# Norms over heads in float32r sums with a logarithm, in place of float32 column sums with Newton steps

## The chip, the cores and the metric

The kernel runs on one core of a Trainium2 chip. Its time is the device time of one execution in microseconds (us), taken as the median of the runs shown; lower is better. A core has five engines that matter here: TensorE (PE in the profile, with its weight loads as PEld), VectorE (DVE), ScalarE (ACT), GpSimd (POOL) and SyncE (SP, which issues most transfers). Each engine runs its own instructions strictly in order.

## The reference

Three layers act on 512 positions of 2048 features in float32. The change lies in the first one, which mixes three kinds of heads, all of 64 features. Cut to what the change touches:

```python
# rwkv: 12 heads, worked in six pairs of 128 features
kk = kk / jnp.maximum(jnp.sqrt(jnp.sum(jnp.square(kk), axis=-1, keepdims=True)), 1e-12)
...                                   # decay, rates a, a recurrence over positions gives y
mu = jnp.mean(y, axis=-1, keepdims=True)
var = jnp.mean(jnp.square(y - mu), axis=-1, keepdims=True)
y = ((y - mu) * lax.rsqrt(var + GN_EPS)) * gn_g + gn_b + bonus
# stick-breaking attention: 12 heads, six pairs
q = _rms(heads(q), qn_g) * (HEAD_DIM ** -0.5)      # x * rsqrt(mean(x*x) + 1e-6) * g
k = _rms(heads(k), kn_g)
# rates of rwkv
logw = -softplus(-(w0 + tanh(wd) @ w_up)) - 0.5;  a = sigmoid(a0 + ad @ a_up)
```

So four times per layer kind a tile of 128 features (two heads) by 512 positions needs one over the root of a sum of squares over 64 features: for the rwkv keys, for the rwkv output's norm, for q and for k of the stick-breaking heads. With six pairs each that is 24 tiles. The other two layers (an S5 layer with chunked attention, and a forgetting attention) are not touched.

## The kernel before

Activations lie with features on partitions and positions along the free axis, so a sum over a head goes across partitions and is done on PE. All large weights (the "dense" products into the tiles `big`) are split in a high and a low float32r part, and each slice of 128 features takes three products (L311, L312, L313) of 128x512. The high part `wh` is a copy on ACT (L181; in some stages on POOL, L280), the low part `wl` a subtraction on DVE (L163). Four slices share a buffer, there are four buffers, and the splitting runs about three buffers ahead of PE.

The order on every engine is the order in which the program emits instructions; no scheduler changes it. Work that isn't dense is written as generators. `pump(n)` takes n steps of the running streams, and one step of the main stream is the three dense products of one slice; `beside(main, side, wait)` lets a side generator do one piece after each step of the main one, from step `wait` on. So a bare `yield` in a side generator stands for "three dense products go in between". Whatever a piece emits for ACT and DVE lands in those engines' queues at that point, behind all that was emitted before.

`head_rs` (L374) is the norm: four float32 products per tile (L383) against the 128x2 matrix `heads` put the sums for 128 positions at a time on partitions; `ops` scales them, `newton` does the inverse root in 10 tiny DVE instructions (L411 to L416), L392 spreads it over 64 columns, and after `lag` steps four transposes (L406) bring it back to the layout of the data, in PSUM; `use` multiplies. It is called at three places:

- `decay` in the start of each rwkv pair (`front`): first the two rates (float32 products `wdad` by `up`, L1403, two Tanh, a scan L1407, two Exp), then the key's norm.
- `norm` of a pair's output, which runs beside the next pair's start; its last act is to add the bonus and write to `yd`.
- `stick_front`: while v is projected, q's and k's norms in one call; v then goes through transposes (L1767).

In an rwkv pair PE then needs, in this order, the products L1493 (keys by queries in chunks), L1525, a triangular inverse that begins at L1652 and goes on at L1662 to L1680, and L1539 and later lines for the state. The inverse's input `xb` comes from two DVE transposes L1641 and L1642 after four ACT copies `xa`. The input of L1539 (`GT`, `KM`, `UV`) comes from ACT copies behind L1493 of the next pair. The key `tm` of the next pair is projected, multiplied on DVE (`tm<-big,rs`), shifted (ACT `omu`, DVE L1355) and squared in between. In a stick-breaking step PE computes scores (L752), ACT and DVE build `sbl` and `sbe` (two Exp, one Ln, L1824 and L1825), PE sums them (L1846), and so on, with the next pair's `stick_front` and dense products pumped in between.

Of the kernel before, what the change touches and what calls it, by code (L numbers as in the profile page):

```python
# [9 lines left out]
F32 = mybir.dt.float32  # L10
F32R = mybir.dt.float32r
I32 = mybir.dt.int32
BF16 = mybir.dt.bfloat16
AF = mybir.ActivationFunctionType
OP = mybir.AluOpType
# [12 lines left out]
EXTRA_RATE = (.4,.5,.5,.5)  # L28
RWKV_WAIT = (5,(2,2,4))
STICK_WAIT = (8,6)  # L30
HEAD_LAG = (3,5,7)
RWKV_STEPS = (0,0,0,(13,6),4,4,3,3,3,1,1)
# [109 lines left out]
class Kern:  # L142
# [49 lines left out]
    def constants(self, tmp):  # L192
# [31 lines left out]
        V = nc.vector  # L224
        V.scalar_tensor_tensor(self.cen_r, blk, -1.0 / 64, self.ident, op0=OP.mult, op1=OP.add)
        self.heads = c.tile([128, 2], F32, name="heads")
        V.tensor_copy(self.heads, blk[:, 0:128:64])
        self.ident_r = mr("ident_r")
        self.copy(self.ident_r, self.ident)
        self.one = c.tile([128, 1], F32, name="one")  # L230
        nc.vector.memset(self.one, 1.0)
# [131 lines left out]
    def small(self):  # L363
        return self.ps.tile([128, 512], F32, name="sm", bufs=4)

    def ring(self, pool, name, bufs):
        return lambda dt=F32: pool.tile([128, T], dt, name=name, bufs=bufs)
# [5 lines left out]

    def head_rs(self, pool, ring, sqs, ops, use, lag=4):  # L374


        nc = self.nc
        V = nc.vector
        n = 8 * len(sqs)
        ps = self.early()  # L380
        for i, sq in enumerate(sqs):
            for b in range(4):
                nc.tensor.matmul(ps[:, 8 * i + 2 * b:8 * i + 2 * b + 2], sq[:, 128 * b:128 * b + 128], self.heads,  # L383
                                 start=True, stop=True)
        small = lambda name, dt=F32: pool.tile([128, n], dt, name=name, bufs=2)
        m = small("hm")
        ops(m, ps[:, 0:n])
        y = self.newton(m, small("hy", I32), small("ht"))
        wide = []
        for i in range(len(sqs)):  # L390
            wide.append(ring())
            V.tensor_copy(wide[i].rearrange("p (g c) -> p g c", c=64),  # L392
                          y[:, 8 * i:8 * i + 8, None].to_broadcast([128, 8, 64]))
        for _ in range(lag):
            yield
        for i, t in enumerate(wide):
            ps = self.early()
            for b in range(4):
                n = slice(128 * b, 128 * b + 128)
                self.spread(ps[:, n], t[:, n])  # L400
            use(i, ps)
            yield
# [971 lines left out]
    def rwkv(self, pool, tm, yd, acts, rs):  # L1374
# [9 lines left out]
        def front(j):  # L1384
# [5 lines left out]
            k = yield from self.shifted(tm, 6 + j, acts, rs)  # L1390
            kk, sq, Pi, P, b = (tm() for _ in range(5))
            self.copy(kk, k, scale=self.pv("k_k", j))
            self.act(sq, kk, AF.Square)
            PT = pool.tile([128, 8], F32, name="PT", bufs=2)

            ks = []

            def decay():

# [4 lines left out]
                for t, ps, bias in zip((Pi, b), both, ("w0", "a0")):  # L1404
                    self.act(t, ps, AF.Tanh, bias=self.half[bias][:, j:j + 1], scale=0.5)
                V.tensor_scalar(Pi, Pi, 0.5, 0.5, op0=OP.mult, op1=OP.add)
                V.tensor_tensor_scan(P, self.reset.rearrange("p c t -> p (c t)"), Pi, 0.0, OP.mult, OP.add)  # L1407
                self.act(Pi, P, AF.Exp, scale=C05)
                self.act(P, P, AF.Exp, scale=-C05)
                yield  # L1410

                def use(_, y):
                    self.mul(kk, kk, y)
                    self.mul(RKV[:, :, 1, 1:64], ch(kk)[:, :, 1:64], ch(P)[:, :, 0:63])
                    V.tensor_copy(RKV[:, :, 1, 0:1], ch(kk)[:, :, 0:1])
                yield from self.head_rs(pool, tm, [sq], lambda m, s: V.tensor_scalar(m, s, 1e-24, None, op0=OP.max), use, HEAD_LAG[0])

# [38 lines left out]
        def norm(j, g, bon, gate):  # L1456
# [5 lines left out]
            gc = self.sums(self.small(), hi, lo, self.cen_r)  # L1462
            yc, sq = tb(), tb()
            self.copy(yc, gc)
            self.act(sq, yc, AF.Square)

# [6 lines left out]
            for _ in range(3):  # L1473
                yield
            yield from self.head_rs(pool, tb, [sq], lambda m, s: V.tensor_scalar(m, s, 1.0 / 64, 64e-5, op0=OP.mult,
                                                                            op1=OP.add), use, HEAD_LAG[1])

# [261 lines left out]
    def stick_front(self, tm, j, acts, rs, pool=None):  # L1739
# [7 lines left out]
        for out, c, gain in ((q, 33 + j, self.qg8), (k, 39 + j, self.pv("kn_g"))):  # L1747
            t = yield from self.projected(tm, c, acts, rs)
            sq = tm()
            self.act(sq, t, AF.Square)  # L1750
            x.append((out, t, gain, sq))

        def use(i, y):
            out, t, gain, _ = x[i]
            V.scalar_tensor_tensor(out, t, gain, y, op0=OP.mult, op1=OP.mult)
            if pool:
# [3 lines left out]
            self.projected(tm, 45 + j, acts, rs),  # L1760
            self.head_rs(self.fr, tm, [y for _, _, _, y in x],
                         lambda m, s: V.tensor_scalar(m, s, 1.0 / 64, 1e-6, op0=OP.mult, op1=OP.add), use, HEAD_LAG[2]), STICK_WAIT[0])

# [171 lines left out]
```

## Time and profile before

| | |
|---|---|
| median of 3 runs | 3011.6 us (3009.29 to 3014.44) |
| the profiled execution | 3016.27 us, of which span 3014.0 us |
| PE busy | 2944.0 us, 98% |
| PEld busy | 2418.0 us, 80% |
| DVE busy | 1619.1 us, 54% |
| ACT busy | 1146.2 us, 38% |
| POOL busy | 373.5 us, 12% |
| mean granted TensorE clock | 0.98 |

The rwkv pairs take about 60 to 600 us of the span, the stick-breaking steps about 600 to 900 us; the norms that change lie there alone. PE is the engine that is hardly ever idle, so time is gained or lost by PE's own work, by what PE waits for, and by the clock that it is granted (1.00 in a row is 2.4 GHz, 0.50 is 1.2 GHz).

### The profile page before, as it was taken

Reading aid. Unit: us, or ns where it says so; the run is one execution under the profiler, and the core shown is the slowest. Engines: PE = TensorE matmul, PEld = TensorE weight load, DVE = VectorE, ACT = ScalarE, POOL = GpSimd, SP = SyncE. Lnnn points to the kernel's source line nnn. Section 1 sums busy time; section 2 is a strip of 40 time slices with the busy share of each in tenths; the row PEclk is TensorE's granted clock in tenths of the full one; section 3 lists DMA queues with packets and bytes.
Section 4 is the critical chain, followed back from the end, with each engine's and each line's share of the span. In section 5 each row is a group of like instructions: output and inputs, shape, how many; then the busy total and the mean of one; then the engine's idle time right before and its main releaser. Section 6 shows DMA issues by size and latency. Waiting matters only on the chain. (4 is left out here: it accounts for less than half of the span.)

```text
span 3014.0 us, 42793 instructions
## 1 busy us (share of the span) xinstructions
PE 2944.0 (98%) x16068; PEld 2418.0 (80%) x16068; DVE 1619.1 (54%) x3253; ACT 1146.2 (38%) x2062; POOL 373.5 (12%) x819
## 2 busy tenths in 40 slices
PE   8999999999999999999999999999999999999998
PEld 6777777778887887788888887888888888888887
DVE  6655555477767675555454455354444444444534
ACT  5443443354454223223344454233333232333432
POOL 0111111013764000211100000001101010100001
PEclk9998999999999999999999999999999999999999
DMA  4211111222234555454433325543332333223443
GB/s 156 67 56 59 57 57 59 78 81 85 94 96 158 158 182 180 135 159 157 138 105 104 102 85 177 146 130 109 101 105 96 98 96 96 95 91 95 148 121 119
DMA packets 195296, 334.01 MB, mean 111 GB/s; under 512 B 29696, under 2 KB 44672, under 8 KB 193936
## 3 DMA queue, kind: packets, MB, share of 16 engines
q1 hardware_dynamic: 193808, 327.08, 34.9%
q0 software_dynamic: 1280, 4.20, 0.4%
q8 instruction: 126, 2.06, 0.3%
q14 instruction: 82, 0.67, 0.1%
HBM read 289.55 MB, written 42.70 MB: 110 GB/s over the span
## 5 line engine op out<-in xcount | busy, mean ns | idle before, releaser
L311 PE MATMUL big<-hi,wh 128*128 128x512 f32 x3424 | 1375.5, 402 | 4.6 <-ACT hi L181 3.9
L312 PE MATMUL big<-lo,wh 128*128 128x512 f32 x3424 | 1347.5, 394 | 2.3 <-DVE lo L163 2.3
L313 PE MATMUL big<-hi,wl 128*128 128x512 f32 x3424 | 1347.0, 393 | 0.7 <-DVE wl L163 0.6
L163 DVE TENSOR_TENSOR wl<-wr,wh 128x512 fp32r<-128x512 f32 x884 | 621.9, 714 | 709.9 <-ACT wh L181 707.6
L311 PEld LDWEIGHTS big<-hi,wh 128*128 128x128 f32 x3424 | 650.1, 190 | 150.2 <-issue 11.1
L181 ACT ACTIVATE wh<-wr 128x512 fp32r<-128x512 f32 x835 | 515.6, 626 | 657.1 <-PE big L312 520.2
L313 PEld LDWEIGHTS big<-hi,wl 128*128 128x128 f32 x3424 | 649.6, 190 | 141.2 <-DVE wl L163 2.7
L312 PEld LDWEIGHTS big<-lo,wh 128*128 128x128 f32 x3424 | 650.8, 190 | 132.8 <-DVE lo L163 5.6
L683 ACT ACTIVATE pm<-pm,mx 128x128 f32<-128x128 f32 (+3 forms) x128 | 70.5, 551 | 178.6 <-DVE mx L679 178.6
L1235 POOL TENSOR_SCALAR dm<-cb,cq 128x128 f32<-128x128 f32 (+1 forms) x64 | 42.4, 663 | 598.4 <-DVE mx L677 580.1
L163 DVE TENSOR_TENSOR tm<-big,rs 128x512 f32<-128x512 f32 x85 | 58.5, 689 | 73.8 <-PE big L313 73.7
L176 ACT ACTIVATE sq<-xn 128x512 f32<-128x512 f32 (+1 forms) x47 | 28.8, 614 | 161.5 <-DVE xn L163 161.5
L181 ACT ACTIVATE pt<-sm 128x512 f32<-128x512 f32 (+3 forms) x96 | 43.4, 526 | 62.7 <-PE sm L711 62.7
L163 DVE TENSOR_TENSOR xn<-big,xr 128x512 f32<-128x512 f32 (+1 forms) x50 | 33.3, 667 | 53.2 <-PE big L313 46.3
L181 ACT ACTIVATE qk<-tm 128x512 fp32r<-128x512 f32 x32 | 20.2, 633 | 96.3 <-DVE tm L163 48.2
L1615 POOL MEMSET xi<- 64x16 f32 x6 | 0.7, 119 | 448.0 <-DVE xi L1614 448.0
L280 POOL CAST wh<-wr 128x512 fp32r<-128x512 f32 x49 | 34.2, 698 | 128.3 <-PE big L312 81.7
L163 DVE TENSOR_TENSOR pl<-sm,pt 128x512 fp32r<-128x512 f32 (+1 forms) x48 | 25.9, 596 | 44.3 <-ACT pt L181 44.3
L689 DVE TENSOR_SCALAR pm<-pm,sm 128x128 f32<-128x128 f32 (+3 forms) x128 | 43.3, 400 | 1.1
L163 POOL TENSOR_TENSOR xn<-xn,rs 128x256 f32<-128x256 f32 x12 | 8.6, 756 | 284.0 <-ACT rs L181 284.0
L1371 DVE SCALAR_TENSOR_TENSOR tm<-big,rs 128x512 f32<-128x512 f32 x33 | 22.7, 689 | 36.5 <-PE big L313 36.5
L311 PE MATMUL sm<-hi,wh 128*128 128x512 f32 x80 | 32.6, 408 | 8.7 <-ACT wh L181 8.7
(449 smaller groups left out, 3118.2 us busy)
## 6 DMA issues: line engine op xcount, KB each, us to landing
wr<-w_in_odd SPq DMA_DIRECT2D x256, 256.0 KB, 3.3
wr<-w_in SPq DMA_DIRECT2D x228, 256.0 KB, 3.1
wr<-w_in_even SPq DMA_DIRECT2D x192, 256.0 KB, 3.5
wr<-w_out SPq DMA_DIRECT2D x64, 256.0 KB, 3.8
wr<-w_out_even SPq DMA_DIRECT2D x64, 256.0 KB, 3.5
wr<-w_out_odd SPq DMA_DIRECT2D x64, 256.0 KB, 3.4
xr<-x SPq DMA_DIRECT2D x48, 256.0 KB, 3.0
yl<-y SPq DMA_DIRECT2D x45, 256.0 KB, 4.2
```

The costliest lines, as they stand in the source:

```text
L163: (eng or self.nc.vector).tensor_tensor(out, a, b, op=op)
L176: self.nc.scalar.activation(out, x, f, scale=scale)
L181: self.nc.scalar.activation(out, x, AF.Copy, scale=scale)
L280: self.nc.gpsimd.tensor_copy(wh, wr)
L311: nc.tensor.matmul(ps, wh[:, i], hi, start=(k == 0), stop=False)
L312: nc.tensor.matmul(ps, wh[:, i], lo, start=False, stop=False)
L313: nc.tensor.matmul(ps, wl[:, i], hi, start=False, stop=(k == n - 1))
L683: nc.scalar.activation(d, d, AF.Exp, bias=mx[:, b:b + 1], accum_out=sm[:, b:b + 1])
L689: V.tensor_scalar(d, d, sm[:, b:b + 1], None, op0=OP.mult)
L1235: nc.gpsimd.tensor_scalar(D[:, QOFF[b]:QOFF[b] + n], cb[:, 0:n], -1.0, cq[:, b, h:h + 1], op0=OP.mult, op1=OP.add)
L1371: self.nc.vector.scalar_tensor_tensor(t, ps, scale, rs, op0=OP.mult, op1=OP.mult)
L1615: G.memset(X.rearrange("p i c -> p (i c)")[:, 0:256:17], 1.0)
```

## The change

`squares` makes, beside the square, its float32r high part (a second ACT instruction). `head_rs` makes the low part on DVE, sums over heads with two float32r products of 128x512 (`sums`) against a 128x128 matrix of ones or of 1/64 per head, so that the sum lies at once on all partitions of its head. The inverse root is exp(-ln(s)/2): ACT Ln from PSUM with the floor as bias (for the keys first a DVE max), ACT Exp, and after the lag one Newton step of three DVE instructions of 128x512, the second of which reads the sums from PSUM. `use` then multiplies by a tile in SBUF. The transposes, the tiny Newton steps and the spread copy are gone. The rates' part of `decay` becomes a generator `rates` that runs between the low part and the sums, in pieces with bare yields. The constants of the layout change with it.

```diff
-RWKV_WAIT = (5,(2,2,4))
-STICK_WAIT = (8,6)
-HEAD_LAG = (3,5,7)
+RWKV_WAIT = (2,(2,2,4))
+STICK_WAIT = (2,6)
+HEAD_LAG = (2,5,8)
...
-        self.heads = c.tile([128, 2], F32, name="heads")
-        V.tensor_copy(self.heads, blk[:, 0:128:64])
+        self.mean_r = mr("mean_r")
+        self.copy(self.mean_r, blk, scale=1.0 / 64)
...
+    def squares(self, ring, x):
+
+        sq, hi = ring(), ring(F32R)
+        self.act(sq, x, AF.Square)
+        self.copy(hi, sq)
+        return sq, hi
+
+    def head_rs(self, ring, sqs, mat, op, floor, use, aside=()):
+
+
+        V = self.nc.vector
+        parts = []
+        for sq, hi in sqs:
+            lo = ring(F32R)
+            self.sub(lo, sq, hi.bitcast(F32))
+            parts.append((hi, lo))
+        yield from aside
+        for _ in range(HEAD_LAG[0]):
             yield
...
+        first = []
+        for (sq, _), (hi, lo) in zip(sqs, parts):
+            first.append((self.sums(self.early(), hi, lo, mat), sq, ring()))
+            yield
+        for ps, y, _ in first:
+            if op == OP.add:
+                self.act(y, ps, AF.Ln, bias=self.floors[floor])
+            else:
+                V.tensor_scalar(y, ps, floor, None, op0=op)
+                self.act(y, y, AF.Ln)
+        for _, y, _ in first:
+            self.act(y, y, AF.Exp, scale=-0.5)
+        for _ in range(HEAD_LAG[len(sqs)]):
+            yield
+        for i, (ps, y, t) in enumerate(first):
+            V.scalar_tensor_tensor(t, y, -0.5, y, op0=OP.mult, op1=OP.mult)
+            V.scalar_tensor_tensor(t, ps, floor, t, op0=op, op1=OP.mult)
+            V.scalar_tensor_tensor(y, t, 1.5, y, op0=OP.add, op1=OP.mult)
+            use(i, y)
             yield
...
-            def decay():
+            def rates():
...
+                yield
+                yield
                 V.tensor_scalar(Pi, Pi, 0.5, 0.5, op0=OP.mult, op1=OP.add)
                 V.tensor_tensor_scan(P, self.reset.rearrange("p c t -> p (c t)"), Pi, 0.0, OP.mult, OP.add)
+                yield
                 self.act(Pi, P, AF.Exp, scale=C05)
                 self.act(P, P, AF.Exp, scale=-C05)
-                yield
-
+
+            def decay():
...
-                yield from self.head_rs(pool, tm, [sq], lambda m, s: V.tensor_scalar(m, s, 1e-24, None, op0=OP.max), use, HEAD_LAG[0])
+                yield from self.head_rs(tm, [sq], self.blk_r, OP.max, 1e-24, use, rates())
...
-            yield from self.head_rs(pool, tb, [sq], lambda m, s: V.tensor_scalar(m, s, 1.0 / 64, 64e-5, op0=OP.mult,
-                                                                            op1=OP.add), use, HEAD_LAG[1])
+            yield from self.head_rs(tb, [sq], self.mean_r, OP.add, 64e-5, use)
```

The compiled programs differ on three engines at the places that matter. First DVE, in the start of the third rwkv pair, where the norm of the pair before (`tb`, `bon`) is used and the next key (`tm`) comes out of its projection. Before:

```order
L392 COPY tb<-hy 128x512
L163 TENSOR_TENSOR wl<-wr,wh 128x512
L163 TENSOR_TENSOR tb<-tb,pa 128x512
L163 TENSOR_TENSOR bon<-bon,tb 128x512
L163 TENSOR_TENSOR bon<-bon,gate 128x512
L163 TENSOR_TENSOR wl<-wr,wh 128x512
L163 TENSOR_TENSOR tm<-big,rs 128x512
```

The same place after the change, from the low part `tb<-tb` on:

```order
L163 TENSOR_TENSOR tb<-tb 128x512
L163 TENSOR_TENSOR wl<-wr,wh 128x512 x2
L412 SCALAR_TENSOR_TENSOR tb<-tb 128x512
L413 SCALAR_TENSOR_TENSOR tb<-pa,tb 128x512
L414 SCALAR_TENSOR_TENSOR tb<-tb 128x512
L163 TENSOR_TENSOR tb<-tb 128x512
L163 TENSOR_TENSOR bon<-bon,tb 128x512
L163 TENSOR_TENSOR bon<-bon,gate 128x512
L163 TENSOR_TENSOR tm<-big,rs 128x512
```

Three instructions of full size stand where a multiplication by PSUM stood, and the key's multiplication still stands behind the last `bon`. Second, ACT at the same place after the change (`floor_136` is the floor of the output norm, `omu` and the two rows behind it belong to the key):

```order
L181 ACTIVATE wh<-wr 128x512
L178 ACT_TABLE_LOAD
L178 ACTIVATE tb<-pa,floor_136 128x512
L176 ACT_TABLE_LOAD
L176 ACTIVATE tb<-tb 128x512
L181 ACTIVATE wh<-wr 128x512 x2
L178 ACTIVATE tb<-tb,pvt 128x512
L181 ACTIVATE tm<-tm,omu 128x512
L181 ACTIVATE tm<-tm,pvt 128x512
L176 ACTIVATE tm<-tm 128x512
L181 ACTIVATE tm<-tm 128x512
```

Before, this place has the rows for `wh`, `tb<-tb,pvt`, `omu`, the key's gain and its Square, and none of the two table loads, the Ln, the Exp and the last copy. In all the program has 31 ACT_TABLE_LOADs before and 67 after. Third, DVE in a stick-breaking step, from the end of the mask on `sbe` to v's projection (the last row). Before:

```order
L163 TENSOR_TENSOR sbe<-sbe,m_lt 128x128
L1755 SCALAR_TENSOR_TENSOR RKV<-tm,qg_152,pa 128x512
L163 TENSOR_TENSOR q_7139<-RKV,q_7139 64x512
L163 TENSOR_TENSOR q_7142<-RKV,q_7142 64x512
L163 TENSOR_TENSOR s5x<-qr_7068 128x32
L163 TENSOR_TENSOR s5x<-qi_7069 128x32
L163 TENSOR_TENSOR tm<-big,rs 128x512
```

After:

```order
L412 SCALAR_TENSOR_TENSOR tm<-tm 128x512
L413 SCALAR_TENSOR_TENSOR tm<-pa,tm 128x512
L414 SCALAR_TENSOR_TENSOR tm<-tm 128x512
L1769 SCALAR_TENSOR_TENSOR RKV<-tm,pvt 128x512
L163 TENSOR_TENSOR kl_5876<-RKV,k_6972 64x512
L163 TENSOR_TENSOR kl_5877<-RKV,k_6976 64x512
L163 TENSOR_TENSOR s5x<-qr_6893 128x32
L163 TENSOR_TENSOR s5x<-qi_6894 128x32
L163 TENSOR_TENSOR tm<-big,rs 128x512
```

Ahead of these nine rows stand the same six for q, and ahead of those the mask on `sbe`. v's multiplication, which stood behind q's use, now stands behind q's and k's use both. Also on DVE, further up in the step, the two low parts `tm<-tm` now stand directly behind the first mask on `sbe`; and on PE q's sums come 12 dense products earlier than the old L383 (12 steps of the order before it, counted in dense products: 1887 against 1899 from the start).

## Rows read from the trace of the kernel before

**Rows 1.** The page: busy time of each engine, share of span, instructions

```profile
PE 2944.0 (98%) x16068; PEld 2418.0 (80%) x16068; DVE 1619.1 (54%) x3253; ACT 1146.2 (38%) x2062; POOL 373.5 (12%) x819
```

**Rows 2.** Waits of PE: engine, line, releaser: us in total, times, longest

```profile
PE pa L383 <- ACT tm L178: 6.6, 5, 2.0
```

**Rows 3.** The old sums by source line: count: least/median/greatest ns, from when to when

```profile
L383 PE MATMUL pa<-heads,tm x144: 165/251/354, 75.6 to 872.5; 128*128 128x2 f32 x144
```

**Rows 4.** Timeline of PE, third rwkv pair: start us, us, instruction, idle before and releaser

```profile
264.66 0.68 PE L1525 MATMUL sm<-UV,GT 64*64 64x64 f32 x16 [1.09 <-ACT UV L181]
...
271.10 0.60 PE L406 MATMUL pa<-ident,tb 128*128 128x128 f32 x4
271.45 0.48 PE L311 MATMUL big<-hi,wh 128*128 128x512 f32 x1
...
278.83 0.39 PE L313 MATMUL big<-hi,wl 128*128 128x512 f32 x1
...
282.36 1.05 PE L383 MATMUL pa<-heads,tm 128*128 128x2 f32 x8 [1.19 <-ACT tm L178]
283.35 1.51 PE L1652 MATMUL sm<-xb,GT 16*32 16x32 f32 x64
```

**Rows 5.** Timeline of DVE, third rwkv pair

```profile
273.31 0.75 DVE L163 TENSOR_TENSOR bon<-bon,tb 128x512 f32<-128x512 f32 x1 [0.88 <-ACT tb L178]
...
275.32 0.68 DVE L163 TENSOR_TENSOR tm<-big,rs 128x512 f32<-128x512 f32 x1
...
281.16 1.03 DVE L1642 STREAM_TRANSPOSE xb<-xa 64x512 f32<-64x512 f32 x1
```

**Rows 6.** Timeline of ACT, first rwkv pair, then the third

```profile
91.38 0.72 ACT L181 ACTIVATE tm<-tm,omu 128x512 f32<-128x512 f32 x1 [1.36 <-DVE tm L163]
...
278.33 0.63 ACT L176 ACTIVATE tm<-tm 128x512 f32<-128x512 f32 x1
```

**Rows 7.** Timeline of ACT, a stick-breaking step: table loads between Exp and Ln

```profile
734.44 1.28 ACT L176 ACT_TABLE_LOAD   x1
735.73 1.28 ACT L176 ACTIVATE sbl<-sbl 128x1280 f32<-128x1280 f32 x1
737.03 1.28 ACT L178 ACT_TABLE_LOAD   x1
```

**Rows 8.** Timeline of PE: inverse and state products of the fifth rwkv pair

```profile
447.11 1.46 PE L1652 MATMUL sm<-xb,GT 16*32 16x32 f32 x64
...
467.35 1.96 PE L1539 MATMUL sm<-KM,GT 64*64 64x128 f32 x32
```

**Rows 9.** Timeline of PE, then DVE, then ACT: the same stick-breaking step

```profile
753.43 1.84 PE L383 MATMUL pa<-heads,tm 128*128 128x2 f32 x16
...
769.76 0.63 PE L1767 MATMUL pa<-ident,tm 128*128 128x128 f32 x4 [1.18 <-DVE tm L163]
...
753.26 0.78 DVE L163 TENSOR_TENSOR sbe<-sbe,m_lt 128x384 f32<-128x384 f32 x2
...
764.04 1.71 DVE L163 TENSOR_TENSOR sbe<-sbe,m_lt 128x384 f32<-128x384 f32 x2
...
768.93 0.69 DVE L163 TENSOR_TENSOR tm<-big,rs 128x512 f32<-128x512 f32 x1
...
751.35 1.28 ACT L176 ACTIVATE sbe<-sbe 128x1280 f32<-128x1280 f32 x1 [2.57 <-DVE sbe L163]
```

**Rows 10.** Windows: from:to, us, busy us of PE, PEld, DVE, ACT, POOL, granted clock

```profile
284.50:300.80 16.30, 16.30 (x140) 12.85 (x136) 8.53 (x25) 3.68 (x6) 0.00 (x0) 0.50 0.18 59
183.00:600.00 417.00, 402.52 (x3597) 316.89 (x3598) 217.36 (x458) 164.64 (x315) 43.94 (x144) 0.93 0.20 61
447.11:467.35 20.24, 20.24 (x280) 16.26 (x279) 12.97 (x31) 8.52 (x14) 0.00 (x0) 0.92 0.20 66
1199.00:1205.00 6.00, 5.59 (x21) 5.23 (x22) 4.29 (x7) 2.23 (x5) 1.12 (x2) 0.50 0.76 259
```

**Rows 11.** Timeline of PE: the resume after one long wait

```profile
1199.41 3.75 PE L1140 MATMUL sm<-U,wt 128*128 128x128 f32 x16 [6.06 <-issue]
```

More of the change, by code (lines that the diff above doesn't have):

```diff
@@ L225, in constants @@
         V.scalar_tensor_tensor(self.cen_r, blk, -1.0 / 64, self.ident, op0=OP.mult, op1=OP.add)
-        self.heads = c.tile([128, 2], F32, name="heads")
-        V.tensor_copy(self.heads, blk[:, 0:128:64])
+        self.mean_r = mr("mean_r")
+        self.copy(self.mean_r, blk, scale=1.0 / 64)
         self.ident_r = mr("ident_r")
         self.copy(self.ident_r, self.ident)
+        self.floors = {}
+        for i, f in enumerate((1e-6, 64e-5)):
+            self.floors[f] = c.tile([128, 1], F32, name="floor%d" % i)
+            V.memset(self.floors[f], f)
         self.one = c.tile([128, 1], F32, name="one")
@@ L372, in silu @@
         self.nc.vector.scalar_tensor_tensor(g, t, 1.0, half, op0=OP.add, op1=OP.mult)
[L374 to L394, printed above, removed]
-            yield
[L396 to L401, printed above, removed]
+    def squares(self, ring, x):
[3 more added lines that the diff above has]
+        return sq, hi
@@ L1390, in front @@
             k = yield from self.shifted(tm, 6 + j, acts, rs)
-            kk, sq, Pi, P, b = (tm() for _ in range(5))
+            kk, Pi, P, b = (tm() for _ in range(4))
             self.copy(kk, k, scale=self.pv("k_k", j))
-            self.act(sq, kk, AF.Square)
+            sq = self.squares(tm, kk)
             PT = pool.tile([128, 8], F32, name="PT", bufs=2)
             ks = []
-            def decay():
+            def rates():
                 both = self.early(), self.early()
@@ L1462, in norm @@
             gc = self.sums(self.small(), hi, lo, self.cen_r)
-            yc, sq = tb(), tb()
+            yc = tb()
             self.copy(yc, gc)
-            self.act(sq, yc, AF.Square)
+            sq = self.squares(tb, yc)
             def use(_, y):
@@ L1748, in stick_front @@
             t = yield from self.projected(tm, c, acts, rs)
-            sq = tm()
-            self.act(sq, t, AF.Square)
-            x.append((out, t, gain, sq))
+            x.append((out, t, gain, self.squares(tm, t)))
         def use(i, y):
@@ L1760, in stick_front @@
             self.projected(tm, 45 + j, acts, rs),
-            self.head_rs(self.fr, tm, [y for _, _, _, y in x],
-                         lambda m, s: V.tensor_scalar(m, s, 1.0 / 64, 1e-6, op0=OP.mult, op1=OP.add), use, HEAD_LAG[2]), STICK_WAIT[0])
+            self.head_rs(tm, [y for _, _, _, y in x], self.mean_r, OP.add, 1e-6, use), STICK_WAIT[0])
         def turn():
```

## The prediction, made before the changed kernel ran

> **What bounds the kernel now.** I read the page's engine row first: PE is busy for 2944.0 of 3014.0 us, no other engine above 54% [rows 1]. So there is little idle time to win on PE, and a change can save only PE's own work, the few waits that it takes away, or clock. Next the waits of PE: the old sums wait for the keys' squares for 6.6 us in all [rows 2]. Third, the windows with the granted clock: over the second to sixth rwkv pair (183 to 600 us) it is 0.93, which is 29 us of lost full-speed work; the longest stretch, behind the third pair's inverse, has 0.50 for 16.3 us and loses half of it, 8.2 us [rows 10]. Last, the timelines of one rwkv pair and one stick-breaking step on three engines [rows 4 to 9]. There the reader is to see that PE, though busy, arrives only about a microsecond before or after what ACT and DVE hand it: L1525 had to wait 1.09 us, the key's sums 1.19 us [rows 4], v's transposes 1.18 us for DVE [rows 9]. These chains have no slack, and the change lengthens them.
>
> **What it removes and adds on PE.** One square took eight passes of the old sums, which occupied PE from 282.36 to 283.35, 0.99 us, and one set of transposes, from 271.10 to 271.45, 0.35 us [rows 4]. The count agrees with [rows 3]: 144 records, of which two stand for a product, are 72 products or 18 tiles (six of keys, twelve of q and k); with the six output norms 24. Two float32r products of 128x512 cost two dense products. Those come every 0.2275 us (0.231 with what stands between them: 33 from 271.45 to 279.15), so 0.455. The saving is 0.885 us a tile, 21 us for 24. It counts only where PE is what everybody waits for.
>
> **What it adds elsewhere.** A norm needs one more ACT copy and one more full DVE subtraction, then a table load, Ln, a table load, Exp on ACT, then three full DVE instructions and a multiplication. A full DVE instruction takes about 0.69, some 0.65 in a row of them, a full ACT one 0.63 [rows 5, 6], a table load 1.28 with the next instruction starting 0.01 us later [rows 7]. The ACT part alone is 1.28 + 0.63 + 1.28 + 0.63 = 3.8 us. The order shows that a load stands before the Ln and another before the Exp at each of the 18 places, which is the 36 more in the count. What goes from DVE (ten tiny instructions of about 0.2 us, a spread copy) is about 2.5 us a norm and what comes about 2.5, so the busy sums say little; the waiting does. Lags of 5 and 8 steps give 15 and 24 dense products, 3.4 and 5.5 us of cover, against an ACT part of 3.8 and (two tiles, 1.28 + 2 x 0.63 twice) 5.1 us and what queues ahead and behind it.
>
> The Trainium skill, page "ScalarE: Activation LUTs", section "Table sets: the hidden batching unit", says that Ln followed by Exp needs one load, as one set holds both. This trace disagrees: in the step of [rows 7] Exp at 735.73 is followed by a load at 737.03 for the Ln behind it. By that rule each norm would have one load, 1.28 us, less; I count it as a rival below. The section "What ACT_TABLE_LOAD costs" of the same page adds about 1.4 us of drain to each load; [rows 7] show none (734.44 to 735.73), so I take none. By that rule each norm's chain would be some 2.8 us longer, an estimate from the page, still the same sign.
>
> **rwkv pairs two to six, first stretch.** I follow the third pair. The copy of the square's high part stands on ACT ahead of GT, UV and KM, which L1525 waits for already, so the second half of L1525 starts 0.55 us later, at 265.2. Then 12 dense products (2.7), the wait for the low part and the sums: about 269.5. Ln and Exp with two loads: 273.4. Two wh copies stand behind them on ACT, and their wl on DVE stand ahead of the Newton step, as the order shows: 275.3. Newton step and multiplication, four of 0.69: 278.1. ACT's gain, DVE's two `bon` instructions (1.5, with 0.88 of waiting for ACT as at 273.31): 280.35. Only then can DVE do `tm<-big` of the next key, which it did at 275.32 [rows 5]: 5.0 us late. From there to the second half of the inverse's input it took 281.16 + 1.03 - 275.32 = 6.87 us; the new copy behind the Square of 278.33 stands ahead of `xa` on ACT, 0.55 more. So L1668 (the old L1652) starts at 280.35 + 6.87 + 0.55 = 287.8, where PE needed it at 283.35 [rows 4]: +4.5 us. PE itself is there at about 281, since it has no key sums to do first; it waits 7 us.
>
> **The same pairs, second stretch.** From the inverse to L1539 it was 20.24 us in the fifth pair [rows 8], at a granted clock of 0.92 [rows 10]: 18.6 at the full one. After the change the key's norm with the rates lies in it. The chain that L1555 (the old L1539) waits for, by the order: fourteen full DVE instructions (low part, wl, wl, Newton step, key, RKV, k2 and its three followers, the gate's `tm<-big` and shift) at 0.65, 9.1; the rates' scaling and scan 1.6; eight full ACT ones at 0.6 (two Exp, Ln, Exp, two wh, gate omu, Tanh), 4.8; two loads, 2.6; the copies of GT, UV and KM, 2.5; and ten handovers between engines at some 0.3. By rows that stand here for full instructions and loads, and estimates from them for the scan, the copies and the handovers, that is 23.5: +4.9. Together 9.4 us a pair, 47 for five. The lost clock of those pairs before is 29 us, 5.8 each. After, the small products behind L1668 remain and long waits stand before them. Between none and the third pair's 8.2 us each [rows 10] I take 3.6, 18 in all, somewhat nearer to the mean before than to none, since part of a slow stretch then falls into a wait. So these pairs cost 47 - 29 + 18 = +36, between +18 and +59.
>
> **First pair.** In the front, r's omu (at 91.38 [rows 6]) and with it the two weight copies behind it wait for a DVE that has the later Newton step and the key's use first. The chain there is again the 5 us of the first stretch, with an extra copy or two, on PE +7. The second stretch as above gives +5, and 3 for the clock: +8. Bounds for both: 0 and 20.
>
> **Stick-breaking, five steps.** The sums for q come 12 dense products (2.7 us) earlier, at 750.7 instead of 753.43 [rows 9]. Their low part stands on DVE behind the mask of 753.26, which waits for Exp at 751.35, and that whole path gets 0.55 us later by the copy of q's high part. Mask to 754.6, low part 0.65: PE stands from 750.7 to about 755.2, 4.5 us. k's sums follow three dense products later, 756.4; loads, two Ln and two Exp take 5 us: 761.4. DVE ends the second mask at about 765, which it did at 764.04 + 1.71 = 765.75, then for q a Newton step and gain (2.7), ACT's copy (0.7), two subtractions (1.4), then for k 2.7, 0.7, and two subtractions with the second's wait (2.0), then v's `tm<-big` at about 776, where it was at 768.93. v's transposes (L1780, the old L1767) start at 776.7, not 769.76: +7 a step, 35 in all. PE's saving in the step (1.8 + 0.7 - 0.9) lies in front of that wait and is lost in it. If DVE is nearer its queue's limit than I think it is +8, if the masks come earlier +4. On the clock: after a wait of 6.06 us [rows 11] it stood at 0.50 for the next 6 us, 3 us lost [rows 10]; a step gets two waits of 4 to 5 us. I take 2 to 2.5 for each, 22 in all less some 2 lost there now: +20, between 0 and 30. The stage: +55, between +20 and +70.
>
> **Sum.** 7 + 8 + 36 + 55 = +106 us on the profiled execution's 3016.27 (the span and 2.27 beside it) gives 3122. That execution lies 4.7 us above the median; on the median of 3011.6 it is 3118.
>
> **Rivals.** (1) The lags cover the chains, and only PE's own work counts: -21, and -7 for the waits of [rows 2]: 2984; with the clock kept up as well, another -29 at most: 2955. It needs the key's `tm<-big` and v's to be no later than now. For it speaks that the extra ACT and DVE work is small against their idle half; against it that both engines are in order and that the order puts three Newton steps and `bon` ahead of those rows. Faster; it decides if the 5 us and 7 us above come out below about 1 each. 7%. (2) The waits are there but the clock doesn't fall in the steps and pairs more than now: 47 + 35 + 12 for the first pair with the dips as they are, less up to 20 where PE's saving shortens a wait: +75, 3085. 18%. (3) Only one of the two stages stalls, the other breaks even: 7 + 8 + 36 = +51 or +55: 3065. 16%. (4) One load a norm, not two, and so about 1.28 us less at some 16 places that lie in a chain: -20, 3098; against it stand [rows 7] and the compiled order. 5%. (5) Every wait is followed by half clock as long as in the third pair: +59 and +70 and the first pair's 20: 3160. 12%. (6) Stalls and savings cancel within 6 us: 2%. My forecast itself: 40%.
>
> **Range.** 3040 to 3180 leaves out (1), (6) and the far end of (5), not over 2 in 10. A measurement of this kernel tells apart about 0.2%, 6 us. Faster by more than that: 0.07, case 1. Within: 0.02, case 6. Slower: 0.91, the rest.
>
> **What would show it.** In the third pair, PE should show a wait of 5 to 8 us before L1668, released by DVE `xb`, and one before L1555; L1668 should come 23 us, not 18, before L1555. In a stick-breaking step a wait of 4 to 5 us should stand before the first sums, released by DVE `tm`, and one of about 5 before L1780, also by DVE `tm`. ACT should be 46 us busier by loads (36 x 1.28) and the clock over the pairs should not be better than 0.93. PE's busy time without its clock should fall by about 21 us. Waits below 2 us at those four lines would make the prediction wrong in its mechanism; waits of that size with the clock at 1.00 would make it wrong in size only, by about 35 us.

## The result and the profile after

The changed kernel takes 3122.6 us in the median (3114.7 to 3130.4), against 3012.3 for the kernel before: a ratio of 1.0367, 95% interval 1.0337 to 1.0396. The forecast was 3118. In the profiled execution the span is 3116.8 us, 102.8 more than before.

The page's engine row of the kernel after, the answer to [rows 1]:

```profile
PE 2943.0 (94%) x15828; PEld 2404.9 (77%) x15828; DVE 1641.2 (53%) x3134; ACT 1237.9 (40%) x2171; POOL 371.1 (12%) x819
```

PE's busy time is the same, its share is 4 points lower: PE waits. Its idle time rose from 70.0 to 173.8 us, by 103.8. That the busy time stayed hides two parts that cancel: summed over windows of 1 us, busy time times what the granted clock lacks to 1.00 is 50.5 us before and 67.3 after, so by this estimate 16.8 us more went to the clock and PE's work at full clock fell by 17.8 (the forecast had about 21). ACT is 92 us busier, half of it the 36 loads (36 x 1.283 = 46). DVE is 22 us busier; neither is near its limit, so the loss can't be seen in their shares. It is in the waits of PE (us in total, times, longest), which answer to [rows 2]:

```profile
PE sm L1668 <- DVE xb L1658: 34.2, 6, 6.9
PE pa L1780 <- DVE tm L163: 33.7, 6, 7.2
PE pa L435 <- DVE tm L163: 23.1, 6, 7.4
PE sm L1555 <- ACT GT L181: 10.2, 5, 3.6
...
PE big L315 <- ACT wh L181: 8.1, 4, 6.9
```

Before, the wait of L1652 was 2.5 us in all and that of L1767 3.1; the old sums L383 waited 8.9 (6.6 of it in [rows 2]), but for ACT; L1539 and L311 (for `wh`, into `big`) had no wait on that list. The third rwkv pair on PE, to be held against [rows 4]; the columns are start, duration, instruction, idle time before and what ended it:

```profile
281.77 0.68 PE L1541 MATMUL sm<-UV,GT 64*64 64x64 f32 x16 [1.09 <-ACT UV L181]
...
285.25 0.39 PE L434 MATMUL pa<-tb,mean_r 128*128 128x512 f32 x1
...
304.74 1.92 PE L1668 MATMUL sm<-xb,GT 16*32 16x32 f32 x64 [6.93 <-DVE xb L1658]
...
328.29 1.10 PE L1555 MATMUL sm<-KM,GT 64*64 64x128 f32 x14 [1.64 <-ACT GT L181]
```

PE's wait of 6.93 us is the end of a chain that starts with the sums. On ACT, at the same place:

```profile
286.36 1.28 ACT L178 ACT_TABLE_LOAD   x1 [2.06 <-PE pa L435]
287.65 0.69 ACT L178 ACTIVATE tb<-pa,floor 128x512 f32<-128x512 f32 x1
288.36 1.28 ACT L176 ACT_TABLE_LOAD   x1
289.65 0.63 ACT L176 ACTIVATE tb<-tb 128x512 f32<-128x512 f32 x1
```

The load begins only when the sums are there, not in the 2 us in which ACT stood idle before them. From there to the key's product on DVE, against [rows 5]:

```profile
292.05 0.68 DVE L412 SCALAR_TENSOR_TENSOR tb<-tb 128x512 f32<-128x512 f32 x1
...
294.22 0.69 DVE L163 TENSOR_TENSOR tb<-tb 128x512 f32<-128x512 f32 x1
...
296.52 0.69 DVE L163 TENSOR_TENSOR bon<-bon,gate 128x512 f32<-128x512 f32 x1
297.13 0.68 DVE L163 TENSOR_TENSOR tm<-big,rs 128x512 f32<-128x512 f32 x1
...
303.57 1.02 DVE L1658 STREAM_TRANSPOSE xb<-xa 64x512 f32<-64x512 f32 x1
```

The key's `tm<-big` starts with the end of the last `bon`, 15.4 us after L1541's second half began at 281.77; before, it took 275.32 - 264.66 = 10.7. That is what I call a convoy: an instruction that was ready (e2 shows it below) waits behind others of another purpose. The same stick-breaking step as in [rows 9], with the fourth pair's v (PE, then DVE, then ACT):

```profile
824.59 0.79 PE L435 MATMUL pa<-tm,mean_r 128*128 128x512 f32 x1 [3.56 <-DVE tm L163]
...
850.64 1.12 PE L1780 MATMUL pa<-ident,tm 128*128 128x128 f32 x4 [7.18 <-DVE tm L163]
...
823.15 0.78 DVE L163 TENSOR_TENSOR sbe<-sbe,m_lt 128x384 f32<-128x384 f32 x2
823.86 1.30 DVE L163 TENSOR_TENSOR tm<-tm 128x512 fp32r<-128x512 f32 x2
...
837.61 0.75 DVE L163 TENSOR_TENSOR sbe<-sbe,m_lt 128x384 f32<-128x384 f32 x2
838.27 0.69 DVE L412 SCALAR_TENSOR_TENSOR tm<-tm 128x512 f32<-128x512 f32 x1
...
844.25 0.69 DVE L412 SCALAR_TENSOR_TENSOR tm<-tm 128x512 f32<-128x512 f32 x1
...
849.90 0.69 DVE L163 TENSOR_TENSOR tm<-big,rs 128x512 f32<-128x512 f32 x1
...
829.55 1.15 ACT L176 ACTIVATE tm<-tm 128x512 f32<-128x512 f32 x2
...
835.17 1.27 ACT L176 ACTIVATE sbe<-sbe 128x1280 f32<-128x1280 f32 x1 [4.47 <-DVE sbe L163]
```

The first sums wait for the low part, which waits for the mask on `sbe`. v's `tm<-big` stands 11.6 us behind the first L412. And the norm's Exp is done at 830.7, while DVE reaches L412 only at 838.27: here the table loads aren't what it waits for. In the five steps the first sums wait 7.42, 4.66, 3.56, 3.57 and 3.63 us, and L1780 waits 4.75, 6.65, 7.18, 7.21 and 7.11. The windows after, against [rows 10] (granted clock is the third column from the end):

```profile
183.00:600.00 417.00, 363.24 (x3386) 281.43 (x3385) 211.61 (x352) 199.10 (x355) 40.05 (x145) 0.92 0.16 54
304.74:328.29 23.55, 21.91 (x278) 17.30 (x278) 14.48 (x25) 12.22 (x19) 0.00 (x0) 0.85 0.14 46
620.00:980.00 360.00, 306.42 (x1377) 249.22 (x1376) 228.54 (x454) 186.72 (x238) 136.79 (x317) 0.91 0.23 75
```

Where the 102.8 us came from, by the start of the same products in both traces:

| stage | from | to | measured | forecast |
|---|---|---|---|---|
| front of the first pair | | L1493 at 99.34, L1509 at 107.21 | +7.9 | +7 |
| first pair | | 175.73, 188.87 | +5.3 | +8 |
| pairs two to six | | L1539 at 543.27, L1555 at 587.21 | +30.8 | +36 |
| stick-breaking, to the last v | | L1767 at 886.87, L1780 at 991.85 | +61.0 | +55 |
| the rest | | end of span | -2.2 | 0 |

These are differences of two single executions. Beyond the last v they come out from -3.1 to +3.9 us in the runs below that keep q's and k's norms in their place, so a few us of a stage mean nothing.

### The profile page after: what moved, and what is told of

The parts are those of the page before. It is cut to its first block, busy times and chain, and to the rows that moved or that the text cites. A ratio compares the mean times of both kernels' runs of the same rounds, so it can differ in the third digit from the quotient of the medians.

```text
span 3116.8 us, 42296 instructions
## 1 busy us (share of the span) xinstructions
PE 2943.0 (94%) x15828; PEld 2404.9 (77%) x15828; DVE 1641.2 (53%) x3134; ACT 1237.9 (40%) x2171; POOL 371.1 (12%) x819
## 5 line engine op out<-in xcount | busy, mean ns | idle before, releaser
L315 PE MATMUL big<-hi,wh 128*128 128x512 f32 x3424 | 1379.2, 403 | 13.1 <-ACT wh L181 8.1
L315 PEld LDWEIGHTS big<-hi,wh 128*128 128x128 f32 x3424 | 653.3, 191 | 161.1 <-issue 11.9
L176 ACT ACTIVATE tm<-tm 128x512 f32<-128x512 f32 (+1 forms) x59 | 36.4, 626 | 29.1 <-DVE tm L163 14.3
L1668 PE MATMUL sm<-xb,GT 16*32 16x32 f32 x384 | 10.8, 229 | 34.2 <-DVE xb L1658 34.2
```

Of the source, the lines that this page charges most:

```text
L176: self.nc.scalar.activation(out, x, f, scale=scale)
L315: nc.tensor.matmul(ps, wh[:, i], hi, start=(k == 0), stop=False)
```

## The experiments

My theory was that in-order queues make the loss: the new norm puts more full-size instructions in a chain, and what stands behind them on DVE and ACT comes late to PE. The rivals were the table loads alone, and the layout numbers alone. Ratios are to the kernel before, measured beside each run; the changed kernel has 1.0367. Its medians there go from 3009.6 to 3012.3 us, so 2 or 3 us between two runs say nothing.

**e1, no table loads.**

```diff
-                self.act(y, ps, AF.Ln, bias=self.floors[floor])
+                self.act(y, ps, AF.Identity, bias=self.floors[floor])
...
-                self.act(y, y, AF.Ln)
+                self.act(y, y, AF.Identity)
```

> Ln is replaced by Identity (so the inverse roots are other numbers than the reference's); every instruction stays in its place, only the 36 added table loads go, 46 us of ACT time. My theory (in-order queues on ACT and DVE, the loads being part of each chain): the wait before L1668 falls from 6.9 to about 4.4 us, that before L1780 from 7.2 to about 4.7, that before the first sums in a stick-breaking step stays near 4.6, since their low part doesn't stand behind a load. About -2.6 us at 5 + 5 places, -1.6 to -2.6 at the second place of five pairs, -3 in the front, some clock: 3122 to about 3080 (3070 to 3095). Rival (the loads are the whole loss, ACT being the limit): about 2990 to 3015, all these waits below 2 us. Rival (loads are hidden): 3122.

Measured 3095.8 us, 1.0292 [1.0275, 1.0309], some 27 us less than the changed kernel: a miss of my number by 16, just outside the range, and both rivals are out. By products' starts the rwkv stage gained 22 us (its excess at the last L1555 fell from 43.9 to 21.5), stick-breaking only 3 (from 61.0 to 58.5). Its waits on PE:

```profile
PE pa L1780 <- DVE tm L163: 31.1, 6, 7.2
PE sm L1668 <- DVE xb L1658: 25.2, 6, 5.1
PE pa L435 <- DVE tm L163: 23.5, 6, 7.4
```

L1668's longest wait fell by 1.8; L1780's not at all. I had put the loads into that chain for this expectation, against the prediction's own working, in which the second mask (765) and not Exp (761.4) came last. The trace after says the same (Exp done 7.6 us before L412).

**e2, the output norm's use later.**

```diff
-        for _ in range(HEAD_LAG[len(sqs)]):
+        for _ in range(lag or HEAD_LAG[len(sqs)]):
...
-            yield from self.head_rs(tb, [sq], self.mean_r, OP.add, 64e-5, use)
+            yield from self.head_rs(tb, [sq], self.mean_r, OP.add, 64e-5, use, lag=14)
```

> Only the lag of the output norm goes from 5 to 14 steps, so that its Newton step and both bon instructions stand on DVE behind tm<-big and xb of the next key. The table loads stay. My theory: tm<-big comes as early as before the change, the wait before L1668 falls from 6.9 to about 2 to 3 us (what is left is the loads and copies ahead of omu on ACT), about -4 us in each of five pairs, so -20, and up to 10 more if the clock recovers: 3122 to about 3100 (3088 to 3108); stick-breaking unchanged. Rival (the loads on ACT hold L1668, not DVE's order): L1668 still waits 5 us or more and the time is 3115 to 3125. Second rival: the norm now lands in the decay's chain and L1555 waits longer by what L1668 saves: 3120.

Measured 3114.9 us, 1.0353 [1.0337, 1.0368]: outside my range, and the interval overlaps that of the changed kernel, so no gain is shown. L1668's wait fell from 34.2 to 1.5 us, more than the theory has it, but a new one took half of that (L1417, 17.1 us at four places), and stick-breaking, which I had expected unchanged, has its excess at 65 instead of 61 (PE waits 6.5 us for k at L766, 2.8 in the changed kernel). PE, ACT and DVE of the third pair:

```profile
300.32 2.07 PE L1417 MATMUL pa<-wdad,up 64*128 64x512 f32 x2 [4.27 <-ACT tm L178]
...
299.60 0.67 ACT L178 ACTIVATE tm<-pa,half_w 128x512 f32<-128x512 f32 x1
...
293.27 0.68 DVE L163 TENSOR_TENSOR tm<-big,rs 128x512 f32<-128x512 f32 x1
...
305.57 0.69 DVE L413 SCALAR_TENSOR_TENSOR tb<-pa,tb 128x512 f32<-128x512 f32 x1
```

The key's `tm<-big` now starts at 293.27, 10.3 us after the second half of L1541 (282.99), as before the change (10.7): it had been ready, and only DVE's order held it. But there are two `pa` buffers in PSUM. The norm's sums keep one until L413 has read them, now at 305.57, so both rates' products share the other, and the second waits until the first Tanh has read the first. The Newton step's look at the sums has a price of its own: it holds PSUM.

**e3, uses of q and k later; e4, their sums later.**

```diff
-HEAD_LAG = (2,5,8)
+HEAD_LAG = (2,5,14)
```

```diff
-STICK_WAIT = (2,6)
+STICK_WAIT = (8,6)
```

> Only the lag of q's and k's norms goes from 8 to 14 steps, so that both uses stand on DVE behind v's tm<-big. My theory: the wait before L1780 (7.2 us) falls below 1.5 us, the wait before the first sums (4.6) stays, and the time falls by 5 x 6 us and up to 8 of clock: 3122 to about 3088 (3080 to 3098). Rival (the stage is bound by the norm chain itself, and q and k are needed right behind v): the wait moves to the scores L766 or to the sums L1859, and the time stays within 3112 to 3130.

> Only the start of q's and k's norms beside v's projection goes back from step 2 to step 8, as it was. It moves the low part and the sums 18 dense products later (4.1 us), and with them both uses behind v's tm<-big. My theory: both waits go, the one before the first sums to below 1 us and that before L1780 to below 1.5, so 5 x (4.2 + 6) = 51 us and most of the stage's 20 us of clock, less what the later q and k cost at the scores, put at 10: 3122 to about 3065 (3055 to 3085). Rival (norm chain bound): the scores L766 wait by what is saved, 3110 to 3125.

Measured 3100.1 us (1.0305 [1.0289, 1.0320]) and 3099.6 us (1.0304 [1.0287, 1.0321]). Both gain some 22 us, e3 two thirds of what I expected and e4 less than half; both times lie above my ranges and below the rivals'. The named waits went or shrank: L1780's is out of e3's list, and in e4 the first sums' fell from 23.1 to 6.9. In their place PE waits for weights, in e3 and, with 20.5, in e4:

```profile
PE big L317 <- DVE wl L163: 20.4, 6, 5.9
```

(This row is e3's.) In e4 there is also L1780, behind L413 (14.7 us): the `pa` buffers again. Where the weights hang shows in e4's step, on ACT, then on DVE, then on PE:

```profile
753.67 1.28 ACT L178 ACT_TABLE_LOAD   x1
754.97 1.27 ACT L178 ACTIVATE tm<-pa,floor 128x512 f32<-128x512 f32 x2
756.25 1.28 ACT L176 ACT_TABLE_LOAD   x1
757.55 1.15 ACT L176 ACTIVATE tm<-tm 128x512 f32<-128x512 f32 x2
758.61 0.61 ACT L181 ACTIVATE wh<-wr 128x512 fp32r<-128x512 f32 x1
...
759.25 0.69 DVE L163 TENSOR_TENSOR wl<-wr,wh 128x512 fp32r<-128x512 f32 x1 [6.70 <-ACT wh L181]
...
772.64 1.29 DVE L163 TENSOR_TENSOR wl<-wr,wh 128x512 fp32r<-128x512 f32 x2
...
773.38 0.50 PE L317 MATMUL big<-hi,wl 128*128 128x512 f32 x1 [3.47 <-DVE wl L163]
```

The convoy only changed its place: 5 us of Ln and Exp on ACT, then DVE's two Newton steps with the uses of q and k (761.97 to 772.61), and behind them, at 772.64, the weight parts for which PE waits.

**e7, the two uses four steps apart,** on top of e4:

```diff
             use(i, y)
-            yield
+            for _ in range(4 if len(sqs) > 1 else 1):
+                yield
```

> As e4 (norms of q and k from step 8), and q's and k's uses four steps apart, so that weight parts wl can go between them on DVE. My theory (one long burst on DVE starves the weights): PE's wait for wl at L317, 20.5 us in e4, falls below 8, and the time from 3100 to about 3085 (3075 to 3095). Rival: the weights wait for wh on ACT, behind Ln, Exp and their loads, and not for the burst; then the wait for weights stays and the time is 3095 to 3110.

Measured 3108.4 us, 1.0323 [1.0294, 1.0351]; the rival holds. PE's wait for DVE's `wl` fell from 20.5 to 4.9 us, but its wait for ACT's `wh` rose from 7.6 to 25.3.

**e5, no last Newton step.**

```diff
-            V.scalar_tensor_tensor(t, y, -0.5, y, op0=OP.mult, op1=OP.mult)
-            V.scalar_tensor_tensor(t, ps, floor, t, op0=op, op1=OP.mult)
-            V.scalar_tensor_tensor(y, t, 1.5, y, op0=OP.add, op1=OP.mult)
```

> The three full DVE instructions of the last Newton step are left out (so the inverse root is only as exact as Ln and Exp make it); all else of the changed kernel stays in place, the table loads too. It tells DVE's share from ACT's. My theory: 2.0 us less per tile in front of what stands behind the uses on DVE. The wait before L1668 falls from 6.9 to about 4.9 us, that before L1555 by up to 2, that before L1780 from 7.2 to about 3.2 (two tiles), that before the first sums in a stick-breaking step stays at 4.6. So -15 in the rwkv pairs, -20 in stick-breaking and -5 of clock: 3122 to about 3082 (3070 to 3095). Rival (ACT with its loads and copies is the last to arrive, DVE has slack): 3110 to 3122.

Measured 3065.7 us, 1.0186 [1.0158, 1.0215]: 57 us less, below my range, about half of the whole loss for 72 instructions of 0.65 us (47 us of DVE time). Its waits:

```profile
PE pa L432 <- DVE tm L163: 25.2, 6, 9.2
PE sm L1665 <- DVE xb L1655: 23.4, 6, 4.8
PE pa L1777 <- DVE tm L163: 11.9, 5, 2.9
```

v's wait (now L1777) fell from 33.7 to 11.9, the inverse's (now L1665) from 34.2 to 23.4, longest 6.9 to 4.8; the first sums' stayed: the waits are as expected, and the time fell further than their sum had it. The edit also takes away the late reader of the sums, L413, that e2 showed to hold a PSUM buffer; but in the changed kernel the only PE wait that names L413 is one of 0.7 us, so there the gain is that of DVE's time. DVE's convoy is shown as the largest single part.

**e6, no Newton step and both placements** (e5 with lag 10 for the output norm and `STICK_WAIT = (8,6)`):

> As e5, without the last Newton step, and in addition both placements: the output norm's lag 10 and the start of q's and k's norms back at step 8. Without the Newton step nobody but Ln reads the sums, so their PSUM buffers come free early, which e2 (L1417 waited for one) and e4 (L1780 waited for L413) lacked. My theory: L1668, L1417 and L1780 wait below 2 us each, the low part's wait goes, wl behind the uses waits less: 3122 - 40 (e5) - 20 - 20 gives about 3045 (3030 to 3070). Rival (ACT's queue with loads and wh copies takes over): 3070 to 3090. A time below 3010 would make the sums in float32r worth having.

Measured 3061.8 us, 1.0173 [1.0148, 1.0197], inside my range, but only 4 less than e5, which the intervals don't tell apart, where I had expected 20. Stick-breaking gained (excess from 31 to 15 us), the rwkv pairs lost 6: with the early rates their two Exp, which wait 2.56 us for the scan on DVE, stand on ACT ahead of the inverse's copy `xb`, and L1675 waits 12.4 us for it at four places. v's L1777, which I had below 2 us, still waits up to 3.1.

**e8, the old layout numbers in the changed method; e9, the same without the Newton step; e10, and the output norm's lag 10; e11, neither loads nor Newton step.** In e8:

```diff
-RWKV_WAIT = (2,(2,2,4))
-STICK_WAIT = (2,6)
-HEAD_LAG = (2,5,8)
+RWKV_WAIT = (5,(2,2,4))
+STICK_WAIT = (8,6)
+HEAD_LAG = (3,5,7)
```

> The changed method with all layout numbers as they were before: waits 5 and 8, lags 3, 5, 7. It tells the method from the numbers. My theory: the method's longer chains cost, whichever of these numbers stand: as e4 in stick-breaking (-22), no gain in the rwkv pairs: about 3100 (3085 to 3120). Rival (the new numbers make the loss, the method is free): 2985 to 3020.

> The changed method without the last Newton step and with all layout numbers as before (waits 5 and 8, lags 3, 5, 7): e5 and e8 in one. My theory: the Newton step lengthens every chain by 2 us a tile and the numbers decide what stands behind it, so both gains hold in large part: 3122 - 57 (e5) - 37 (e8) = 3028, at worst 20 less of a gain where both shorten one wait: 3028 to 3048, PE's wait for wl at L317 below 8 us. Rival (e5 and e8 shorten the same waits): 3055 to 3066.

> As e9, and the output norm's lag 10, so that its use stands behind the next key's tm<-big and xb. With the old numbers the rates and the key's norm lie behind the inverse's start, so there is room. My theory: L1668's wait (36 us in e8) goes below 10, 10 to 20 us less than e9: about 3015 (3000 to 3035). Rival (the Ln and Exp with their loads stand ahead of omu on ACT and hold xb): no more than 5 us less than e9.

> Neither table loads (Identity in place of Ln, so other numbers than the reference's) nor the last Newton step, the changed layout numbers. It asks whether the two parts add up. My theory (both lie in series in the same chains): 3122 - 27 - 57 = 3038 (3030 to 3050), and what is left above 3012 is the order alone: the first sums' wait for the low part (25 us in e5) stays as it is. Rival (either alone already uncovers the next limit): 3052 to 3066. Rival (order costs nothing): below 3000.

Measured: e8 3085.7 us, 1.0243 [1.0216, 1.0271], so the numbers are a third of the loss and the method the rest. e9 3027.1, 1.0063 [1.0046, 1.0080]; e10 3016.1, 1.0023 [1.0010, 1.0037]; both within 2 us of what was expected (the inverse's wait in e10 is 10.6 us in all, a little above the 10 named), so the Newton step's gain and that of the numbers add up. e11 3048.6, 1.0130 [1.0110, 1.0150]: without loads and Newton step, but with the changed numbers, 37 us of loss against 3012 are left. PE's waits there for DVE's low part (25.4), the inverse's input (13.8) and v (10.4) say where; that it is the order of the rest is argued from them, and not tried by a further edit on e11. The loads are worth 17 us there, not 27, so part of the two gains looks like one and the same wait.

**e12, the old norm where the new one still lost.** The old `head_rs` for q and k and for the first pair's key, the new one without the Newton step, with e10's numbers, elsewhere:

```diff
-                yield from self.head_rs(tm, [sq], self.blk_r, OP.max, 1e-24, use, rates())
+                if j:
+                    yield from self.head_rs(tm, [sq], self.blk_r, OP.max, 1e-24, use, rates())
+                else:
+                    for _ in rates():
+                        pass
+                    yield
+                    yield from self.head_rs_small(pool, tm, [sq], lambda m, s: V.tensor_scalar(m, s, 1e-24, None, op0=OP.max), use, 3)
```

> The old norm where e10 still lost (q and k in stick-breaking, and the key of the first pair, whose front has no other work to hide a long chain), the new one without its last Newton step and with the later output norm in the rest: five keys and six output norms. The mean's 1/64 moves into Ln's scale. My theory: the stages stand alone, so e10's rwkv pairs (11 us ahead of before at the last L1552, though 7 behind in the front) and the old stick-breaking add up: 3012 - 11 - 5 = 2996 (2988 to 3004), with L1665's waits as in e10 (about 10 us in all) and the granted clock over the pairs 0.97 or better. Rival (the rwkv gain comes from clock that the longer first stage leaves, or the first stick-breaking step loses it again as in e10, where 8 us went between the first and the second pair's v): 3004 to 3014.

Measured 3007.8 us, 0.9988 [0.9978, 0.9998]: just below the kernel before, by 0.1%, and in the rival's range. By stages of the two profiled executions, which differ by 9.4 us where the medians differ by 1.9: the front is even (+0.8), the last L1539 comes 15.1 us earlier than before, v of the first stick-breaking pair 15.5, that of the second 9.7, and there it stays. The windows over the pairs, the kernel before first, show the granted clock (0.94, then 0.97), and below them PE's wait in the first stick-breaking step:

```profile
190.00:600.00 410.00, 395.94 (x3563) 311.28 (x3562) 214.76 (x446) 161.76 (x308) 38.42 (x126) 0.94 0.20 61
...
190.00:600.00 410.00, 385.32 (x3505) 299.17 (x3504) 208.54 (x369) 213.21 (x369) 40.94 (x136) 0.97 0.21 66
```

```profile
591.14 0.79 PE L793 MATMUL sm<-q,k 128*128 128x512 f32 x1 [4.35 <-ACT k L181]
...
588.50 1.28 ACT L181 ACTIVATE q<-RKV 64x512 fp32r<-64x512 f32 x2 [3.58 <-DMA y<-bon]
```

What the pairs gained is mostly clock. From the second pair's L1493 to the last L1539 they take 352.8 us, 14.8 less than before; summed over windows of 0.5 us, busy time lost 10.2 us to the clock there, 27.3 before, while PE's work at full clock is 5.5 us less and its idle time 7.9 more. Why the clock is better isn't shown.

ACT's copies of q and k wait there; the profile names the write of the last pair's `bon` as what they wait for, and the later norm may delay that write. Whether the last pair's norm should keep its short lag for this reason was not tried.

## Why the prediction was right, and where it was off

- The first stretch of the pairs held, step by step. From the second half of L1541 the forecast had `tm<-big` 15.15 us later (280.35 from 265.2) and L1668 22.6 later; measured 15.36 and 22.97. Against before that is 4.7 and 4.3 us, and 0.65 more came ahead of it (8.35 us from L1509 to there, 7.70 before), where the forecast had 0.55. PE waits 6.93 us where 7 was forecast, 6.9 in four of the five pairs and 5.8 in the last.
- The second stretch held in length: 23.5 us forecast from L1668 to L1555, measured 23.28, 23.55, 23.40, 23.62 and 21.74 in the five pairs. But the chain is only just what PE waits for: L1555 waits 1.64 us in four pairs, in the last not at all, the one of the four lines named under "What would show it" that stays below 2 us. Of the third pair's 23.55 us PE is busy for 21.91.
- What that length costs depends on the same stretch before, and there I mixed the clock up. It took 21.72, 26.20, 21.72, 20.24 and 19.15 us; in the third pair, which I had followed, it became 2.65 us shorter. From the second to the sixth pair the cost is 3.4, 2.3, 7.8, 8.4 and 9.0 us. I took all 29 us of lost clock off and put 18 on again. Summed over windows of 0.5 us, busy time in these pairs lost 27.3 us before and 27.0 after. What the longer chain covers is only the 17 us that lay in the five second stretches: 47 - 17 = 30, measured 30.8. The half clock behind L1668 after the change lies in front of a wait; in the third pair at most 1.3 us of it reached the chain (DVE stands 1.28 us for PE's L1680 at 315.61).
- Stick-breaking held in its mechanism and nearly in size: waits of 4.5 and 5 us forecast, 3.56 to 7.42 and 4.75 to 7.21 measured. The clock's 20 us were right: from the last L1555 to the last L1780 busy time lost 21.8 us to it, and 1.7 over the same products before. The mean of 0.91 over 360 us would give 32, but part of that lies in waits, where it costs nothing, as in this window with no product in it:

```profile
843.50:850.50 7.00, 0.00 (x0) 0.00 (x0) 5.52 (x9) 3.14 (x5) 2.96 (x12) 0.81 0.20 75
```

- So the 6 us by which that stage is over its forecast lie in the chains: PE's idle time grew by 52.5 us there, its work at full clock fell by 11.6, and that leaves 41, or 8.2 a step, where the forecast had 7.
- The front (+7.9) hung, as forecast, on the weight copies behind omu on ACT: L315 waits 6.9 us for `wh` at 98.47. The first pair's second stretch grew by 3.6 us (22.86 to 26.48), less than the 5 taken.
- That the total came within 5 us of the median's forecast is in part luck: the pairs were put 5 us too high and stick-breaking 6 too low.
- One reading was slightly off: 33 products from 271.45 to 279.15 are 0.233 us each, not 0.231. It changes nothing.
- What the sum had no term for is how the cost divides. The forecast spoke of loads and Newton steps as parts of one chain; taken out alone they give 27 and 57 us, taken out together 74 (e11), and some 37 are left. PE's work did fall, by 17.8 us over the whole run, but in the changed kernel its waits outweigh that several times over.
- Rival (4), one load a norm, is out: the trace after has a load before the Ln (286.36) and another before the Exp (288.36). The rule of the Trainium skill, page "ScalarE: Activation LUTs", section "Table sets: the hidden batching unit", would have one load there, and this trace doesn't agree. The drain of the same page's section "What ACT_TABLE_LOAD costs" isn't seen after either: 0.01 us between load and Ln.

## What to carry to other kernels

Work that is moved from PE to half-idle engines is paid where those engines' queues stand in front of something that PE needs: look, in the order, for what stands behind the new instructions, not at the busy shares. Count everything that a late reader holds: a later instruction that reads PSUM again kept a buffer, and a fix of the order alone turned one wait into another. When a chain is too long, cut instructions out of it first and then move it: here moves alone gave from 8 us, which the intervals don't show, to 37, the cut 57, and both together 61 (e6) to 106 (e10) of 110, by which moves they were. Before a longer chain is priced by one pair, look at the same stretch in all of them: in the third pair, where it had run at half clock, the longer chain cost 2.3 us, in the sixth 9.0.

## What the runs showed of the hardware

Whether a table load can hide in idle time depended on what its ACTIVATE waited for. In the row at 286.36 the Ln reads sums that PE writes in PSUM, and the load starts only when they are there, though ACT was idle for 2.06 us before; at the six output norms 15.0 us of ACT's idle time end so. Where the operand came from DVE, the load ran ahead of it. In e2, the key's norm on ACT, then the max on DVE that writes the Ln's operand:

```profile
309.15 1.28 ACT L176 ACT_TABLE_LOAD   x1
310.64 0.63 ACT L176 ACTIVATE tm<-tm 128x512 f32<-128x512 f32 x1 [0.21 <-DVE tm L405]
...
309.93 0.68 DVE L405 TENSOR_SCALAR tm<-pa 128x512 f32<-128x512 f32 x1
```

The load is under way 0.78 us before that max begins. Why the two differ isn't shown.

After the waits of PE of 3.56 us (824.59), 6.90 (98.47) and 6.93 (304.74) the granted clock is at the lower level for a while: behind 824.59 it is 0.50 over the next 4.5 us, and dense products follow each other every 0.43 us where the full clock has 0.23.
